# A scheduler's model of TensorE: other prices for weight matmuls and for fp32 matmuls

## The chip, the cores and the metric

The kernel is one program on one core of a Trainium2 chip. The metric is device time in microseconds, the median of three runs: 2716.33 before (2714.63 to 2718.19). The profile comes from an execution of its own, which took 2712.5 us, with a span of 2710.6 us from the first to the last instruction; of the difference of 1.9 us the records show nothing.

## What is computed

Two blocks run one after the other on 256 tokens of width 1024, with 256 context tokens in the first block. Cut to its outline (`silu` and the norms as usual):

```python
for i in range(2):                       # first block: two layers
    x, ctx = ffn(x), ffn(ctx)            # SwiGLU, hidden width 2816, half residual, adaptive norms
    if i == 0:
        oc, ox = deltanet(ctx, x)        # gated delta rule, 8 heads, chunks of 64, both directions
    else:
        oc, ox = window_attention(ctx, x)
    x = ffn(x + gate * ox)               # ctx too, in layer 0
u = rms_norm(x)                          # second block
proj = u @ w_in                          # one wide projection for three branches
y = gates * (conv_branch, ssd_branch, window_attention_branch)
x = x + merged(y) @ w_mix_out
x = x + cross_attention(rms_norm(x), norm(mem))     # keys and values from 256 memory tokens
x = x + relu(rms_norm(x) @ w_up)**2 @ w_down        # hidden width 4096
```

In the DeltaNet, each chunk of 64 needs the solution of a unit lower triangular system (`triangular_solve` in the reference).

## The kernel before

All weights are read once from HBM. Each product with a weight is made in three matmuls in fp32r (`mm3`): weight and activation are each split into a high and a low part, and high x high, high x low and low x high are added in PSUM. ScalarE makes the high part of a weight chunk and VectorE the low part (`split_w`: `CAST t<-raw` and `TENSOR_TENSOR t<-raw,t`). An fp32r matmul has 512 columns where context and tokens go together, 256 where there are tokens alone. Other matmuls, of the mixers, are in plain fp32; the trace shows two records for each of them.

**The order is made by a scheduler in the program** (`Driver`), while the program is built. Every engine has a clock in a table, `self.t`. Each instruction goes through `Engine.__getattr__`, line 191, which takes a price from `Engine.cost` and lets `Clocks.run` move the engine's clock; all instructions therefore stand at line 191 in the profile, and all DMAs at line 237, on one queue of SyncE that works in order. Work is written as generators ("streams") with priorities. `Driver.run` takes `now`, the clock of TensorE, and advances the first stream whose condition holds and whose `ready` time is not past `now`. Streams with `bg` (the splits, the substitution `dn_steps`, the convolution's `conv_taps`, rows of the modulation) go on while the clock of their own engine is at most 0.5 us ahead of `now`. Where no stream can go on, a job is taken: a piece of weight matmuls (`acc`, `tok_jobs`, `halves`). So jobs fill the time in which the streams wait, and the price of a matmul decides how many of them stand ahead of the next stream. Where there is neither, and `hot` is set, `keep_busy` issues a matmul of `ones` with the identity that serves nothing but the clock of TensorE; in `Clocks.run` a matmul costs double after a window with few columns.

**The stages of the trace**: start until 44 us, a feed-forward until 405, the DeltaNet until 868, feed-forwards until 1604, window attention until about 1764, a feed-forward until 1964, the three branches until about 2450, cross attention until 2521, the MLP until 2710.

Three places matter below.

- **DeltaNet.** `dn_prep(h)` stores the chunk matrices of a head to a scratch tensor in HBM (`ld`). `dn_subst(b)` loads those of four heads into a tile `bx` and starts `dn_steps(b)`, 62 VectorE instructions that solve four heads at once (`n<-bx,bx` and `bx<-bx,n`): block 0 for heads 0 to 3, block 1 for heads 4 to 7. `dn_store` writes the result to `xd`, from where `dn_head(h)` loads it (four DMAs a head, `t<-xd` and `t<-ld`) and goes on with small matmuls; `dn_chain` and `dn_out` run along the chunks of one head and direction, with VectorE instructions such as `s<-ps,dn_cKV`, and `out_jobs` multiplies with the output weight. In the middle `mem_norm` loads the memory tokens (`memT`), norms them, and `mem_k` offers 192 weight matmuls of 256 columns, for the cross attention much later, as filling work.
- **Window attention.** `tok_jobs` projects tokens; `att_q(j,t)` transposes queries that ScalarE, VectorE and GpSimd have normed and rotated.
- **Branches.** `conv_taps` runs the convolution's taps on VectorE (`xres<-t,c_late,xres`, two taps a step), `ssd_group(g)` prepares and `ssd_pair(g,j)` multiplies the state space branch; its factors come from VectorE (`t<-t,t` 128x512).

Of the kernel before, what the change touches and what calls it, by code (L numbers as in the profile page):

```python
# [106 lines left out]
class Clocks:  # L107
# [16 lines left out]
    def run(self, e, cost, ins, outs):  # L124

        rows = ins[0].shape[0] / P if ins else 1
        start = self.t[e]
        ins = [r for r in (region(a) for a in ins) if r]
        outs = [r for r in (region(a) for a in outs) if r]
        for rs, write in ((ins, False), (outs, True)):  # L130
            for tag, p0, p1, b0, b1 in rs:
                for q0, q1, c0, c1, t, f, w in self.log.get(tag, ()):
                    if (w or write) and q0 < p1 and p0 < q1 and c0 < b1 and b0 < c1:
                        start = max(start, t + self.hop(f, e))
        if e == "PE":

            tick = int(start / TICK)
            self.cols[tick] = self.cols.get(tick, 0) + cost * 2400 * rows
            if self.cols.get(tick - 1, 0) < 3060:
                cost *= 2  # L140
        self.t[e] = end = start + cost
        for rs, write in ((ins, False), (outs, True)):
            for tag, p0, p1, b0, b1 in rs:
                old = self.log.get(tag, ())
                keep = [o for o in old if not (p0 <= o[0] and o[1] <= p1 and b0 <= o[2] and o[3] <= b1
                                               and (write or not o[6] and o[5] == e))]
                self.log[tag] = keep[-40:] + [(p0, p1, b0, b1, end, e, write)]
        return end


class Engine:
# [5 lines left out]
    def cost(self, op, a, k):  # L157
        def size(ap):
            n = 1
            for s in ap.shape[1:]:  # L160
                n *= s
            return n

        n = size(k.get("out", a[0] if a else None))
        if self.name == "PE":
            if op == "transpose":
                return 0.12
            if a[2].dtype == F32R:
                return 0.0025 + max(n * 0.000417, 0.107)

            tiles = {32: 0.29, 64: 0.52}.get(a[0].shape[0], 1) if a[1].shape[0] == P else 1
            return 2 * max(n * 0.000833, 0.03) * tiles
        if self.name == "ACT":
            c = 0.093 * (1 + sum(hasattr(k.get(x), "tensor") for x in ("scale", "bias"))) + n * 0.000833
            f = k.get("func")
            if f in TABLES and not self.drv.has(f):
                self.drv.table = AF.Exp if f == AF.Tanh else f
                c += 1.28
            return c
        if self.name == "DVE":  # L180
            if op == "reciprocal":
                return 0.07 + n * 0.0063
            c = 0.061 * sum(hasattr(k.get(x), "tensor") for x in ("scalar", "scalar1", "scalar2"))
            return 0.068 + c + (size(k["in_"]) if op == "tensor_reduce" else n) * 0.00104
        return 0.1 + n * 0.0021
# [2911 lines left out]
```

## Time and profile before

| | us |
|---|---|
| median of three runs | 2716.33 |
| the profiled execution | 2712.5 |
| its span | 2710.6 |
| TensorE matmuls busy | 2633.4 (97%) |
| VectorE busy | 1928.1 (71%) |
| ScalarE busy | 1255.8 (46%) |
| GpSimd busy | 101.2 (4%) |
| mean granted clock of TensorE | 0.983 |

Engines work beside each other, so shares do not add up. A row of a timeline gives the start, the time from the first start to the last end, the instruction and how often; a bracket at its end is idle time of the engine ahead of it and what ended that. The chain of waits is followed back from the last instruction. The granted clock is 1 at 2.4 GHz and 0.5 at 1.2 GHz.

### The profile page before, as it was taken

What the parts mean: (1) busy time and instruction counts of PE and PEld (TensorE: products, weight loads), DVE (VectorE), ACT (ScalarE), POOL (GpSimd) and SP (SyncE); (2) the same over time, 40 slices, a digit from 0 to 9 for tenths busy, and PEclk for the clock granted to TensorE, in tenths of its full rate; (3) what the DMA queues carried; (4) which work ended last, traced back from release to release, by engine and by line L of the source; (5) the groups of instructions that cost most, each with busy time, mean ns of one, the idle gap of its engine ahead of it and who ended that gap; (6) DMA issues with size and microseconds to landing.
All of it is one profiled execution on the core that took longest, in us unless ns stands there. A gap on an engine that the chain in (4) does not pass through costs nothing.

```text
span 2710.6 us, 45364 instructions
## 1 busy us (share of the span) xinstructions
PE 2633.4 (97%) x17414; PEld 2330.9 (86%) x17414; DVE 1928.1 (71%) x3897; ACT 1255.8 (46%) x2799; POOL 101.2 (4%) x114
## 2 busy tenths in 40 slices
PE   7999999999789999999999998999999899999999
PEld 5888888887779888889888886899979789999999
DVE  6878767897768498875433367765688898886763
ACT  4323145754245323234423255654476676565652
POOL 0000000200010000000000001000010220000000
PEclk8999999999789999999999998999999999999999
DMA  8657723759433465672322221355554444554554
GB/s 317 210 195 261 253 94 124 243 185 263 121 122 110 150 214 206 241 248 78 111 100 93 93 101 55 105 195 183 173 170 155 150 170 159 182 191 150 179 194 134
DMA packets 194058, 452.57 MB, mean 167 GB/s; under 512 B 33472, under 2 KB 78624, under 8 KB 193840
## 3 DMA queue, kind: packets, MB, share of 16 engines
q1 hardware_dynamic: 193840, 449.66, 49.6%
q8 instruction: 137, 2.24, 0.3%
q14 instruction: 81, 0.66, 0.1%
HBM read 418.65 MB, written 30.94 MB: 166 GB/s over the span
## 4 chain that ended last, share of the span: by engine, by line
PE 90%; DVE 6%; ACT 2%; issue 1%; DMA 1%; POOL 0%; SPq 0%; DVEq 0%; POOLq 0%; ACTq 0%
PE ps L191 90%; DVE t L191 3%; ACT t L191 1%; DVE n L191 1%; DVE rs L191 1%; DVE s L191 1%; ACT s L191 1%; DVE xres L191 0%; DMA row<-in_ada_w 0%; DVE bx L191 0%; DMA xres<-in_xT 0%; ACT L191 0%; ACT n L191 0%; DVE acc L191 0%; DVE ps L191 0%
## 5 line engine op out<-in xcount | busy, mean ns | idle before, releaser
L191 PE MATMUL ps<-t,t 128*128 128x256 f32 (+4 forms) x14610 | 2373.5, 326 | 22.2 <-DVE t L191 13.3
L191 PEld LDWEIGHTS ps<-t,t 128*128 128x128 f32 (+2 forms) x14610 | 2077.4, 188 | 273.1 <-issue 25.8
L191 DVE TENSOR_TENSOR t<-raw,t 128x512 fp32r<-128x512 f32 x1124 | 735.4, 684 | 60.5 <-ACT t L191 54.2
L191 ACT CAST t<-raw 128x512 fp32r<-128x512 f32 x1124 | 630.3, 610 | 254.3 <-DMA raw<-in_ffn_w 188.3
L191 ACT CAST t<-t 128x512 fp32r<-128x512 f32 (+2 forms) x144 | 68.2, 493 | 426.6 <-DVE t L191 426.1
L191 DVE TENSOR_TENSOR t<-t,ps 128x512 f32<-128x512 f32 (+1 forms) x104 | 64.7, 628 | 234.4 <-PE ps L191 234.4
L191 DVE CUSTOM_DVE_ANT_0 t<-row,bx,c_early 128x1024 bf16<-128x1024 f32 x128 | 163.9, 1280 | 47.9 <-DMA row<-in_ada_r 47.4
L191 DVE SCALAR_TENSOR_TENSOR xres<-ps,modG,xres 128x256 f32<-128x256 f32 x216 | 97.2, 479 | 117.1 <-PE ps L191 116.3
L191 ACT ACTIVATE t<-ps 128x512 f32<-128x512 f32 (+3 forms) x161 | 75.0, 466 | 195.7 <-PE ps L191 182.7
L191 POOL TENSOR_TENSOR t<-t,c_late 128x512 f32<-128x512 f32 (+2 forms) x58 | 67.1, 1172 | 1715.2 <-ACT t L191 1094.9
L191 DVE CUSTOM_DVE_ANT_0 row<-row,bx,c_early 128x1024 f32<-128x1024 f32 x96 | 122.7, 1280 | 1.2
L191 DVE TENSOR_TENSOR t<-t,t 128x512 fp32r<-128x512 f32 (+4 forms) x174 | 95.1, 561 | 39.4 <-ACT t L191 38.9
L191 DVE SCALAR_TENSOR_TENSOR t<-ps,c_late,t 128x254 f32<-128x254 f32 (+3 forms) x176 | 111.9, 637 | 12.8 <-ACT t L191 7.3
L191 PE MATMUL ps<-s,t 128*128 128x128 f32 x512 | 87.7, 315 | 22.1 <-ACT t L191 10.0
L191 PEld LDWEIGHTS ps<-s,t 128*128 128x128 f32 x512 | 73.4, 215 | 32.6 <-ACT t L191 10.9
L191 ACT COPY t<-ps 128x512 f32<-128x512 f32 (+4 forms) x141 | 57.8, 435 | 93.5 <-PE ps L191 88.1
L191 DVE SCALAR_TENSOR_TENSOR xres<-t,c_late,xres 128x256 f32<-128x256 f32 x150 | 87.5, 583 | 3.1
L191 ACT ACT_TABLE_LOAD x58 | 74.4, 1283 | 2.7 <-PE ps L191 1.7
L191 PE MATMUL ps<-c_early,t 128*128 128x128 f32 (+1 forms) x374 | 59.9, 285 | 10.4 <-ACT t L191 6.0
L191 PEld LDWEIGHTS ps<-c_early,t 128*128 128x128 f32 (+1 forms) x374 | 43.7, 145 | 26.0 <-ACT t L191 13.6
L191 ACT ACTIVATE n<-xres 128x256 f32<-128x256 f32 x90 | 35.7, 414 | 59.8 <-DVE xres L191 58.4
L191 ACT ACTIVATE t<-ps,c_late 128x256 f32<-128x256 f32 (+1 forms) x64 | 37.6, 588 | 53.7 <-PE ps L191 53.6
(188 smaller groups left out, 1365.3 us busy)
## 6 DMA issues: line engine op xcount, KB each, us to landing
raw<-in_ffn_w SPq DMA_DIRECT2D x240, 512.0 KB, 4.2
row<-in_ada_r SPq DMA_DIRECT2D x128, 512.0 KB, 4.4
raw<-in_w_in SPq DMA_DIRECT2D x81, 512.0 KB, 3.5
raw<-in_dn_w SPq DMA_DIRECT2D x33, 512.0 KB, 4.0
raw<-in_w_up SPq DMA_DIRECT2D x32, 512.0 KB, 4.2
raw<-in_w_down SPq DMA_DIRECT2D x32, 512.0 KB, 5.5
raw<-in_ffn_w SPq DMA_DIRECT2D x32, 384.0 KB, 3.6
s<-t SPq DMA_DIRECT2D x32, 256.0 KB, 4.2
```

The costliest lines, as they stand in the source:

```text
L191: r = f(*a, **k)
```

## The change

Two formulas in `Engine.cost` get other numbers. In the scheduler's prices (not measured times) an fp32r matmul goes from 0.216 to 0.231 us at 512 columns and from 0.109 to 0.119 at 256, an fp32 matmul of 128 columns from 0.213 to 0.219, one of 32x32 from 0.060 to 0.055, and one of one column from 0.060 to 0.040.

```diff
@@ Engine.cost, engine PE
             if a[2].dtype == F32R:
-                return 0.0025 + max(n * 0.000417, 0.107)
+                return 0.006 + max(n * 0.0004395, 0.1)
             tiles = {32: 0.29, 64: 0.52}.get(a[0].shape[0], 1) if a[1].shape[0] == P else 1
-            return 2 * max(n * 0.000833, 0.03) * tiles
+            return 2 * max(n * 0.000855, 0.02) * tiles
```

No work is added or taken away but two of the matmuls of `keep_busy` (34 instead of 32). Only the order moves, and with it the buffers. Three places follow, each as it stands before and then as it stands in the change.

SyncE's queue in the DeltaNet, before, after the store of block 0's solution (`xd<-bx`); `ld_126` and `ld_127` are blocks 0 and 1 of the scratch tensor, and the rows behind it are the loads of heads 0 to 3, and after them `bx<-ld_127`.

```order
L237 DMA xd_128<-bx_4875 128x32x32
L237 DMA t_5778<-in_memT 128x512
L237 DMA t_5780<-in_memT 128x512
L237 DMA t_5782<-in_memT 128x512
L237 DMA t_5784<-in_memT 128x512
L237 DMA z_153<-t_5776 128x512
L237 DMA ld_127<-t_5741 128x4x128
L237 DMA ld_127<-t_5742 128x4x128
L237 DMA q_144<-t_5202 128x512
L237 DMA q_145<-t_5203 128x512
L237 DMA t_5809<-xd_128 128x4x128
L237 DMA t_5812<-xd_128 128x4x128
```

In the change, twelve loads of heads 0 to 2 and four weight loads and stores later, this piece begins with the fourth head.

```order
L237 DMA raw_5785<-in_xk_w 128x1024
L237 DMA t_5791<-xd_128 128x4x128
L237 DMA t_5794<-xd_128 128x4x128
L237 DMA t_5795<-ld_126 128x4x128
L237 DMA t_5796<-ld_126 128x4x128
L237 DMA t_5807<-in_memT 128x512
L237 DMA t_5809<-in_memT 128x512
L237 DMA t_5811<-in_memT 128x512
L237 DMA t_5813<-in_memT 128x512
L237 DMA z_153<-t_5805 128x512
L237 DMA ld_127<-t_5822 128x4x128
L237 DMA ld_127<-t_5823 128x4x128
```

The four loads of `memT` have moved from ahead of all sixteen loads of the heads to behind them. The load `bx<-ld_127` comes 36 rows into the piece that begins with the store in the change (26 before), behind six loads of head 0's later tiles that it had ahead of it before.

VectorE in the substitution of block 1, before: `n` and `bx` are its rows, `s` and `t` those of the chains of heads 0 to 3.

```order
L191 TENSOR_TENSOR n_6354<-bx_5954,bx_5955 128x192
L191 TENSOR_TENSOR bx_5955<-bx_5955,n_6354 128x24x8
L191 SCALAR_TENSOR_TENSOR s_6506<-ps_6491,dn_cA,t_5814 128x128
L191 TENSOR_SCALAR s_6510<-ps_6479,dn_cKV 128x128
L191 TENSOR_TENSOR n_6353<-bx_5954,bx_5955 128x207
L191 TENSOR_TENSOR bx_5955<-bx_5955,n_6353 128x23x9
L191 TENSOR_TENSOR n_6354<-bx_5954,bx_5955 128x220
L191 TENSOR_TENSOR bx_5955<-bx_5955,n_6354 128x22x10
L191 TENSOR_SCALAR t_5838<-ps_6316 64x4x64
L191 TENSOR_TENSOR n_6353<-bx_5954,bx_5955 128x231
L191 TENSOR_TENSOR bx_5955<-bx_5955,n_6353 128x21x11
L191 TENSOR_TENSOR n_6354<-bx_5954,bx_5955 128x240
```

In the change, from the same step (128x192) on:

```order
L191 TENSOR_TENSOR n_6201<-bx_6045,bx_6046 128x192
L191 TENSOR_TENSOR bx_6046<-bx_6046,n_6201 128x24x8
L191 TENSOR_SCALAR t_5772<-ps_6173 64x4x64
L191 TENSOR_SCALAR s_6375<-ps_6322,dn_cKV 128x128
L191 SCALAR_TENSOR_TENSOR t_5764<-ps_6219,dn_eg,t_5764 128x128
L191 TENSOR_TENSOR t_5764<-ps_6219,t_5764 128x128
L191 COPY n_5970<-ps_6357 32x128
L191 COPY n_5970<-ps_6358 32x128
L191 SCALAR_TENSOR_TENSOR t_5764<-ps_6263,dn_eg,t_5764 128x128
L191 TENSOR_TENSOR t_5764<-ps_6263,t_5764 128x128
L191 SCALAR_TENSOR_TENSOR s_6394<-ps_6381,dn_cA,t_5748 128x128
L191 SCALAR_TENSOR_TENSOR s_6398<-ps_6391,dn_cA,t_5761 128x128
```

Rows of the chains now stand between the steps in greater number. Between the first step of block 1 and its last stand 105 rows before and 166 in the change, 61 of them steps in both: 55 rows more of the chains of heads 0 to 3 and five more splits; after the last step 73 rows of those chains are left before, and 18 in the change. On TensorE, the filling matmuls of `mem_k` stand otherwise to the substitution of block 1: before, 102 of the 192 ahead of its first step, 39 between first and last and 51 behind (3 of these before the last instruction of the DeltaNet); in the change 12, 87 and 93 (45).

VectorE in the branches, before, ahead of the first factor of `ssd_pair` of group 0, which is the row `t_20963<-t_20963,t_20834`:

```order
L191 TENSOR_TENSOR t_21067<-raw_20907,t_21066 128x512
L191 SCALAR_TENSOR_TENSOR xres<-t_19925,c_late,xres 128x256 x2
L191 TENSOR_TENSOR t_21085<-raw_20953,t_21084 128x512
L191 TENSOR_TENSOR t_21108<-raw_20953,t_21107 128x512
L191 SCALAR_TENSOR_TENSOR xres<-t_19925,c_late,xres 128x256 x2
L191 TENSOR_TENSOR t_21133<-raw_21046,t_21132 128x512
L191 SCALAR_TENSOR_TENSOR xres<-t_19925,c_late,xres 128x256 x2
L191 TENSOR_TENSOR t_21158<-raw_21046,t_21157 128x512
L191 SCALAR_TENSOR_TENSOR xres<-t_19925,c_late,xres 128x256 x2
L191 TENSOR_TENSOR t_20963<-t_20963,t_20834 128x512
```

In the change, ahead of the same factor, here `t_20940<-t_20940,t_20829`:

```order
L191 SCALAR_TENSOR_TENSOR t_21024<-ps_20979,c_late,t_21024 128x255
L191 TENSOR_TENSOR t_21040<-raw_20879,t_21039 128x512
L191 TENSOR_TENSOR t_21058<-raw_20921,t_21057 128x512
L191 SCALAR_TENSOR_TENSOR t_21024<-ps_21019,c_late,t_21024 128x253
L191 SCALAR_TENSOR_TENSOR t_21024<-ps_21019,c_late,t_21024 128x254
L191 SCALAR_TENSOR_TENSOR t_21024<-ps_21019,c_late,t_21024 128x255
L191 TENSOR_TENSOR t_21084<-raw_20921,t_21083 128x512
L191 TENSOR_TENSOR t_21107<-raw_20977,t_21106 128x512
L191 TENSOR_TENSOR t_20940<-t_20940,t_20829 128x512
L191 TENSOR_TENSOR t_20943<-t_20943,t_20829 128x512
```

The four tap steps are gone from there: in both orders 30 tap rows are issued ahead of this factor, but in the change the last of them stands 31 rows ahead of it. What is left next to the factor are splits and the branch's own short convolution (`t<-ps,c_late,t`). Between this factor and the first one of group 1 stand 24 rows before and 35 in the change: six more splits, three more rows of the short convolution, two more tap rows.

## Rows read from the trace of the kernel before

**Rows 1.** The page: busy time of two engines' groups, and the chain of waits.

```profile
PE 2633.4 (97%) x17414; PEld 2330.9 (86%) x17414; DVE 1928.1 (71%) x3897; ACT 1255.8 (46%) x2799; POOL 101.2 (4%) x114
...
PE 90%; DVE 6%; ACT 2%; issue 1%; DMA 1%; POOL 0%; SPq 0%; DVEq 0%; POOLq 0%; ACTq 0%
```

**Rows 2.** TensorE by form: count, busy us, mean ns, idle before.

```profile
L191 PE MATMUL ps<-t,t 128*128 128x512 f32 x5448 | 1262.5, 392 | 0.6 <-ACT n L191 0.6
L191 PE MATMUL ps<-t,t 128*128 128x256 f32 x8136 | 1026.3, 287 | 8.1 <-DVE t L191 5.7 <-ACT t L191 2.2
```

**Rows 3.** Busy time by stretch: length, PE, PEld, DVE, ACT, POOL, granted clock, DMA.

```profile
50.00:100.00 50.00, 50.00 (x279) 43.89 (x278) 41.34 (x68) 16.33 (x30) 0.00 (x0) 1.00 0.67 247
...
667.70:707.90 40.20, 29.55 (x279) 26.88 (x278) 34.49 (x108) 9.82 (x31) 2.13 (x2) 0.76 0.26 88
707.90:813.00 105.10, 89.63 (x910) 78.73 (x909) 69.40 (x227) 45.90 (x168) 9.02 (x9) 0.88 0.45 139
813.00:868.40 55.40, 55.22 (x343) 49.01 (x343) 46.99 (x112) 29.77 (x77) 3.69 (x4) 1.00 0.31 105
1640.00:1703.00 63.00, 53.47 (x346) 36.34 (x344) 44.41 (x94) 32.57 (x78) 10.04 (x12) 0.89 0.12 42
```

**Rows 4.** Timeline of TensorE in the DeltaNet, around the norm of the memory.

```profile
615.79 4.47 PE L191 MATMUL ps<-t,t 128*128 128x512 f32 x19
620.10 1.05 PE L191 MATMUL ps<-t 128*128 128x128 f32 x8
...
622.58 9.13 PE L191 MATMUL ps<-c_early,ones 128*128 128x128 f32 x34
...
636.72 3.55 PE L191 MATMUL ps<-t,t 128*128 128x256 f32 x15
```

**Rows 5.** Timeline of SyncE's DMA queue, same place.

```profile
618.99 0.43 SPq L237 DMA_DIRECT2D xd<-bx  x1
619.51 5.78 SPq L237 DMA_DIRECT2D t<-in_memT  x4
...
629.50 1.45 SPq L237 DMA_DIRECT2D t<-xd  x2
...
643.36 0.83 SPq L237 DMA_DIRECT2D bx<-ld  x1
...
649.71 3.04 SPq L237 DMA_DIRECT2D t<-s  x4
```

**Rows 6.** Timeline of VectorE: the first step of block 1.

```profile
667.66 0.18 DVE L191 TENSOR_TENSOR n<-bx,bx 128x31 f32<-128x31 f32 x1
```

**Rows 7.** VectorE by form, 640 to 812 us: three forms of the chains, the splits.

```profile
L191 DVE TENSOR_SCALAR s<-ps,dn_cKV 128x128 f32<-128x128 f32 x45 | 15.0, 343 | 6.5 <-PE ps L191 6.3
...
L191 DVE TENSOR_TENSOR t<-ps,t 128x128 f32<-128x128 f32 x39 | 11.2, 287 | 1.9 <-ACT t L191 1.0
...
L191 DVE TENSOR_TENSOR t<-raw,t 128x512 fp32r<-128x512 f32 x12 | 8.0, 676 | 2.2 <-ACT t L191 2.2
```

**Rows 8.** Timeline of TensorE in the window attention.

```profile
1649.16 1.09 PE L191 MATMUL ps<-c_early,t 128*128 128x128 f32 x4 [4.37 <-DVE t L191]
...
1665.88 1.33 PE L191 MATMUL ps<-c_early,t 128*128 128x128 f32 x8 [0.96 <-ACT t L191]
1668.92 3.34 PE L191 MATMUL ps<-t,t 64*128 64x512 f32 x14 [1.72 <-DVE t L191]
```

**Rows 9.** Timeline of TensorE in the branches: groups 0 and 1 of `ssd_pair`.

```profile
2134.93 0.71 PE L191 MATMUL ps<-t,t 128*64 128x128 f32 x6 [3.63 <-DVE t L191]
...
2155.43 0.68 PE L191 MATMUL ps<-t,t 128*64 128x128 f32 x6 [3.28 <-issue]
```

**Rows 10.** Timeline of VectorE in the branches: two tap steps.

```profile
2122.06 2.41 DVE L191 SCALAR_TENSOR_TENSOR xres<-t,c_late,xres 128x256 f32<-128x256 f32 x2
...
2133.27 1.00 DVE L191 SCALAR_TENSOR_TENSOR xres<-t,c_late,xres 128x256 f32<-128x256 f32 x2
```

**Rows 11.** Timeline of GpSimd beside those taps: its first row.

```profile
2122.02 0.74 POOL L191 TENSOR_TENSOR n<-n,t 128x256 f32<-128x256 f32 x1 [92.87 <-ACT n L191]
```

## The prediction

> **What bounds the kernel now.** The page comes first: matmuls are busy for 2633.4 of 2710.6 us, and the chain of waits, followed back from the end, lies on TensorE for 90%, on VectorE for 6% [rows 1]. The forms then say what TensorE does: 5448 matmuls of 512 columns and 8136 of 256 are nearly all of it, and they hardly wait (0.6 and 8.1 us in all) [rows 2]. The busy time by stretch says where order can matter at all. In a feed-forward stretch TensorE is busy 50.00 of 50.00 us at a granted clock of 1.00 [rows 3]; there another order of the same matmuls costs nothing as long as it stays full, and some 2200 us are of this kind. The rest is a few stretches: the DeltaNet from the end of its projections at 620.1 to 868.4 (busy 29.55 of 40.20 and 89.63 of 105.10 us, at clocks of 0.76 and 0.88), the window attention (53.47 of 63.00, at 0.89) [rows 3], and two waits in the branches (3.63 and 3.28 us) [rows 9]. Only there can the change move the end.
>
> No instruction becomes faster. The pace itself can be read off: 19 matmuls of 512 columns from 615.79 take 4.47 us, the last for 0.392, so their starts are (4.47 - 0.392) / 18 = 0.227 us apart [rows 2, 4]. The old price was 0.216, the new one is 0.231; the new one is nearer. That alone is worth nothing: an order is paid for by the waits that it leaves.
>
> The Trainium skill speaks against the change at this point. "TensorE: Matmul & The Clock Gate", section "Wait — 56ns, not 53.3ns?", gives 215.7 ns from start to start for 512 columns, which is the old price. By it the new table would be the worse one and I would put ten points more on slower, while the sum would stay, since the order is fixed when the program is built. The trace has 227 ns, so the measurement decides for the new price.
>
> **The change, part by part.**
>
> *DeltaNet.* Before, the queue of SyncE stores block 0's solution at 618.99, spends 5.78 us on the memory tokens, and comes to the first load of a head at 629.50 and to block 1's load at 643.36. TensorE meanwhile has 34 records of `ones` matmuls from 622.58, and the first `mem_k` matmuls come at 636.72 [rows 4, 5]. In the change the heads' loads go first and the memory norm comes behind them. So heads 0 to 3 start earlier, the filling starts later, and block 1's substitution meets other neighbours. Heads 4 to 7 wait for that substitution, and the stage's end waits for them, so I follow it in three terms.
>
> (a) Its first step, now at 667.66 [rows 6]. Ahead of it 90 `mem_k` matmuls are gone from TensorE, at 1026.3 / 8136 = 0.126 us each 11.3 us [rows 2]; nine splits are gone from VectorE, at 0.676 us each 6.1 us [rows 7]. Against that, block 1's load stands behind six more loads on SyncE, four of which take 3.04 us, so six some 4.6 [rows 5]. From -11 to +5; I take -6, the splits, because the step is a VectorE instruction and those were in its own queue.
>
> (b) Its length, now 667.7 to 707.9. The 55 rows more of heads 0 to 3 are forms of 0.287 to 0.343 us, at 0.327 on average 18.0 us, and five splits are 3.4, together 21.4 [rows 7]. VectorE is busy for 34.49 of these 40.20 us, so at most 5.7 us of it find idle time [rows 3]: from +16 to +21. I take +18: some of the idle time is a wait for TensorE that stays.
>
> (c) What follows it, 707.9 to 868.4. The same 55 rows of VectorE are missing there: -18.0 if VectorE set the pace. TensorE loses 65 matmuls of the chains; an fp32 matmul of 128 columns is two records at 1.05 / 8 = 0.13 us [rows 4], so 17.1 us, and gets 42 more `mem_k` matmuls, 5.3 us: -11.8. If heads 4 to 7 only wait for their own chains, nothing comes back. From -18 to 0; TensorE is busy there for 89.63 + 55.22 of 160.5 us, VectorE for 69.40 + 46.99 [rows 3], so I take TensorE's figure: -12.
>
> Together -6 + 18 - 12 = 0, and with the ends that hurt or help at once -11 + 16 - 18 = -13, or +5 + 21 - 9 = +17, where (c) returns half of VectorE's figure.
>
> *Window attention.* Before, TensorE is full until 1644.8, then waits 4.37 us for the transposes of `att_q` [rows 8]. In the change these transposes stand two groups of three matmuls earlier. The wait begins 6 x 0.227 = 1.4 us earlier and ends when it did, and these six come behind it. They are lost if nothing later waits, and found again if they fill the waits of 0.96 and 1.72 us that follow [rows 8]. From -1 to +4 (a longer wait can bring the half clock once more; the stretch has 0.89 already [rows 3]). I take +1.4.
>
> *Branches.* Before, the factor of `ssd_pair` in group 0 stands on VectorE behind four tap steps of two taps, the last of which starts at 2133.27, and TensorE waits 3.63 us for it until 2134.93 [rows 9, 10]. The change puts all four steps ahead of the preparation of the group. If the factor then comes a wait earlier, -3.6. But VectorE is nearly full there, and a tap step put earlier pushes what stood there. In group 1 eleven more rows stand ahead of the factor, six splits of 0.676 and five short ones, some 6 us in VectorE's queue, against 3.28 us of wait now [rows 7, 9]: +3, from 0 to +6. Together -0.6, from -4 to +5.
>
> A tap step takes 2.41 us while GpSimd works, from 2122.02 on, and 1.00 us after it has ended [rows 10, 11]. The Trainium skill, "SBUF — State Buffer", section "SBUF: two separate sides", names a port pair of the two engines that one of them holds for a whole instruction. By it steps moved ahead of GpSimd's run would cost 1.0 each, and three of them would save VectorE 4 us; the sum for the branches would be about -4. No row shows when the moved steps will run, so I leave it at the bound.
>
> *The rest.* Two more `keep_busy` matmuls stand where TensorE waits anyway: nothing. The norms between the stages start some matmuls later, in full stretches: nothing, and the waits behind them stay.
>
> **Sum.** 0 + 1.4 - 0.6 = +0.8 us: from the profiled 2712.5 to 2713.3, and since the median of the runs stands 3.8 us above the profiled one, 2717. That is no change that a measurement of this kernel can tell, which takes some 0.2%, 5.4 us.
>
> **The rivals.**
>
> *Tail relieved, faster.* Heads 0 to 3 use the hole from 622 to 637 and are done when heads 4 to 7 start. For it: all of the work of (c) is really gone from the tail, filling lies beside it, and the clock there is only 0.88. Against it: heads 4 to 7 depend on block 1, which (b) delays. With all low ends in the DeltaNet, -13, and the rest as above: 2716.3 - 12 = 2704.
>
> *Block 1 pays in full, slower.* If its load is late by the loads ahead of it and its 62 steps share VectorE with the chains throughout, (a) is +5, (b) +21, (c) only -9: +17, 2716.3 + 18 = 2734. For it: VectorE is busy 86% there. It decides from a first step later than about 666, with a last step later than 725.
>
> *The waits only change places, slower by a little.* Window attention and group 1 take their upper ends (+4 and +6, with nothing won in group 0): 2716.3 + 10 = 2726. For it: both lie behind engines whose work did not shrink.
>
> *Nothing moves that counts.* The order differs in names of buffers and in filling alone, and the waits last what they did: 2716. It ends as the forecast does, and is counted with it.
>
> **How the numbers follow.** Forecast, with the last rival: 0.38. Relieved tail: 0.30. Block 1 in full: 0.20. Waits change places: 0.12. So faster 0.30, same 0.38, slower 0.32. The range reaches to the time of either far rival and two or three us beyond, since either can fall on both sides of its figure: 2701 to 2736. The forecast's own range is 2711 to 2722, the bound of 5.4 us on either side.
>
> **What would show it.** (a) The first small `n<-bx,bx` row, at about 662 where this is right. (b) The last one some 58 us later, about 720. (c) From it to the end of the stage about 150 us instead of 160. In the window attention the wait ahead of the four transposes at about 5.7 instead of 4.37 us. In the branches no wait of over a microsecond ahead of group 0, and one of 3 to 6 us ahead of group 1. The feed-forward stretches should stay at 50.00 of 50 us. I am wrong if one of these shows a gap, or if block 1's substitution ends earlier than before: then VectorE had more room than its busy share says.

## The result, and the profile after

The changed kernel takes 2752.1 us (2751.07 to 2754.76, four runs) against 2715.48 before (2713.93 to 2718.19): a ratio of 1.0132 [1.012, 1.0144], 36.6 us slower. The forecast was 2717, its range ended at 2736, and the truth lies outside. The profiled execution took 2754.76 us, 2.7 above the median, where that of before stood below its own; so the two traces differ by 42.3 us in span, somewhat more than the medians.

The page of the changed kernel, busy time and the chain of waits, which answer to [rows 1]:

```profile
span 2752.9 us, 45377 instructions
...
PE 2657.6 (97%) x17418; PEld 2352.0 (85%) x17418; DVE 1921.0 (70%) x3897; ACT 1259.8 (46%) x2803; POOL 102.8 (4%) x114
...
PE 55%; issue 31%; DVE 8%; ACT 3%; DMA 3%; SPq 0%; POOL 0%; DVEq 0%; ACTq 0%; POOLq 0%
```

Two sums can be read off. TensorE's idle time is span less busy time: 77.2 us before, 95.3 now, so 18.1 of the 42.3 us are new waits. The other 24.2 us are busy time, with the same number of matmuls but four: the work did not grow, it ran longer, and the mean granted clock fell from 0.983 to 0.971. Where it fell differs by stage, as the stretches below show. In the chain, "issue" has 31% instead of 1%; it names no culprit, and idle rows tell more.

TensorE by form, as in [rows 2]:

```profile
L191 PE MATMUL ps<-t,t 128*128 128x512 f32 x5448 | 1269.6, 393 | 9.3 <-ACT t L191 8.3 <-DVE t L191 1.0
L191 PE MATMUL ps<-t,t 128*128 128x256 f32 x8136 | 1031.8, 287 | 7.2 <-DVE t L191 3.9 <-ACT t L191 3.1
```

The matmuls of 512 columns waited 0.6 us in all before and wait 9.3 now. That is the first surprise: most of them belong to the feed-forwards, the full stretches. Busy time by stretch, as in [rows 3] (length, PE, PEld, DVE, ACT, POOL, clock, DMA share, GB/s); first the feed-forward after the DeltaNet and 50 us out of it, then the DeltaNet up to block 1's first step, its steps, and what follows, then the window attention, and last the whole DeltaNet behind its projections and a piece of it:

```profile
880.00:1258.10 378.10, 369.08 (x1782) 311.47 (x1781) 281.38 (x496) 112.91 (x216) 0.00 (x0) 0.99 0.56 196
1100.00:1150.00 50.00, 43.58 (x182) 35.21 (x181) 40.80 (x72) 13.17 (x24) 0.00 (x0) 0.93 0.64 228
625.80:670.00 44.20, 38.50 (x358) 32.62 (x357) 26.38 (x66) 15.57 (x46) 2.17 (x2) 0.58 0.96 273
670.00:730.70 60.70, 54.23 (x503) 50.91 (x503) 51.79 (x169) 20.08 (x62) 2.08 (x2) 0.83 0.21 70
730.70:880.00 149.30, 141.13 (x1201) 123.94 (x1200) 103.65 (x288) 70.89 (x231) 12.73 (x12) 0.89 0.45 140
1640.00:1703.00 63.00, 53.70 (x259) 38.39 (x259) 40.92 (x82) 33.56 (x86) 10.28 (x14) 0.92 0.22 76
...
625.80:880.00 254.20, 233.86 (x2058) 207.47 (x2057) 181.82 (x520) 106.53 (x337) 16.98 (x16) 0.82 0.48 147
633.20:670.70 37.50, 33.09 (x299) 28.67 (x300) 22.16 (x56) 13.12 (x42) 2.17 (x2) 0.50 0.91 259
```

The same two stages in the trace of before, the feed-forward and the DeltaNet:

```profile
868.40:1233.70 365.30, 365.30 (x1790) 310.05 (x1789) 283.24 (x498) 114.63 (x216) 0.00 (x0) 1.00 0.59 203
622.70:868.40 245.70, 217.55 (x2029) 190.63 (x2028) 180.70 (x514) 107.69 (x336) 17.32 (x16) 0.90 0.49 148
```

In the DeltaNet TensorE does not wait longer, it waits less: length less busy time is 28.2 us before and 20.3 now. Its busy time rose by 16.3 us, two thirds of the 24.2, for nearly as many records (2029 and 2058), and the clock fell from 0.90 to 0.82. From 633.2 to 670.7 it was at half clock throughout, busy for 33.09 of 37.50 us with the small matmuls of the heads and, until 656.9, without a weight matmul. So this stage pays in clock and not in waits.

The feed-forward after the DeltaNet, full before from end to end (365.30 of 365.30 us), has 9.02 us of gaps. Where most of them are, by TensorE's timeline:

```profile
976.95 0.50 PE L191 MATMUL ps<-t,t 128*128 128x512 f32 x1 [1.94 <-ACT t L191]
...
1083.82 26.45 PE L191 MATMUL ps<-t,t 128*128 128x512 f32 x116
1116.33 0.80 PE L191 MATMUL ps<-t,t 128*128 128x512 f32 x1 [6.06 <-ACT t L191]
```

The releaser is ScalarE's `t`; back from it, on ScalarE and VectorE:

```profile
1115.66 0.62 ACT L191 CAST t<-t 128x512 fp32r<-128x512 f32 x1 [8.64 <-DVE t L191]
```

```profile
1101.29 1.28 DVE L191 CUSTOM_DVE_ANT_0 t<-row,bx,c_early 128x1024 bf16<-128x1024 f32 x1 [2.55 <-DMA row<-in_ada_r]
...
1110.27 1.28 DVE L191 CUSTOM_DVE_ANT_0 t<-row,bx,c_early 128x1024 bf16<-128x1024 f32 x1 [0.47 <-DMA row<-in_ada_r]
...
1113.73 1.28 DVE L191 CUSTOM_DVE_ANT_0 t<-row,bx,c_early 128x1024 bf16<-128x1024 f32 x1 [0.23 <-DMA row<-in_ada_r]
...
1114.94 0.68 DVE L191 TENSOR_TENSOR t<-t,ps 128x512 f32<-128x512 f32 x1
```

So a load of the modulation's weights (`row<-in_ada_r`) is late; VectorE stands 2.55 us at an instruction that nobody is in a hurry for; behind it in the same queue stands the feed-forward's product (`t<-t,ps`), which ends at 1115.62; ScalarE casts it, and TensorE, out of other work, has waited 6.06 us. The page gives those loads 4.1 us from issue to landing (before: 4.4). The scheduler's price for 512 KB is 0.5243 MB at 360 GB/s, 1.46 us, plus `DMA_LAT`, 0.75 us: 2.2 us.

### The profile page after: what moved, and what is told of

Same layout as the page of the kernel before. It is cut to its first block, busy times and chain, and to the rows that moved or that the text cites. A ratio compares the mean times of both kernels' runs of the same rounds, so it can differ in the third digit from the quotient of the medians.

```text
span 2752.9 us, 45377 instructions
## 1 busy us (share of the span) xinstructions
PE 2657.6 (97%) x17418; PEld 2352.0 (85%) x17418; DVE 1921.0 (70%) x3897; ACT 1259.8 (46%) x2803; POOL 102.8 (4%) x114
## 4 chain that ended last, share of the span: by engine, by line
PE 55%; issue 31%; DVE 8%; ACT 3%; DMA 3%; SPq 0%; POOL 0%; DVEq 0%; ACTq 0%; POOLq 0%
PE ps L191 55%; DVE t L191 4%; ACT t L191 2%; DVE rs L191 1%; DVE n L191 1%; ACT L191 1%; DMA row<-in_ada_r 1%; DVE xres L191 1%; DVE bx L191 0%; DMA t<-xd 0%; DVE s L191 0%; DVE row L191 0%; DMA t<-band 0%; DMA raw<-in_ffn_w 0%; DMA raw<-in_ada_w 0%
## 5 line engine op out<-in xcount | busy, mean ns | idle before, releaser
L191 PE MATMUL ps<-t,t 128*128 128x256 f32 (+3 forms) x14610 | 2392.3, 328 | 42.2 <-DVE t L191 19.1
L191 DVE CUSTOM_DVE_ANT_0 t<-row,bx,c_early 128x1024 bf16<-128x1024 f32 x128 | 164.1, 1282 | 72.7 <-DMA row<-in_ada_r 72.5
L191 ACT ACTIVATE s<-ps,dn_cV 128x128 f32<-128x128 f32 x64 | 22.7, 369 | 81.6 <-DVE s L191 64.8
```

The costliest lines, as they stand in the source:

```text
L191: r = f(*a, **k)
```

## The experiments

The tables below give, for each kernel, its time, that of the kernel before on the same chip, and by how much each stage is longer than in the trace of before (us, worked out from the first and the last weight matmul of the stages). Lengths before: the first feed-forward with the projections of the DeltaNet 586.5, the DeltaNet behind them 245.7, the feed-forward after it 365.3, window attention 129.7, the branches up to their gates 298.4, and on to the cross attention 188.7. "Rows" is VectorE's whole wait for `row<-in_ada_r`. In the first two columns of stages part of a difference is scatter: e17 and e18 have the old order word for word up to the branches, and show up to 7.5 us in the one and 4.2 in the other, but at most 1.1 in the next two. Most kernels ran once, and 19 executions of the kernel before on one chip took 2709.28 to 2728.68 us; so a difference of less than some 10 us between two single times says little, and the stages say more.

In the expectations, **M** (margin) says that the too cheap matmul kept the other engines ahead of TensorE; **F** that the fp32 price does it; **R** (rough) that the old order is a good one among many and any other loses; **L** (landing) that the loads' price is too low and the cheap matmul covered for it.

| kernel | time | before | first ffn, proj. | DeltaNet | ffn after | window | branches | on | rows |
|---|---|---|---|---|---|---|---|---|---|
| before | | | | | | | | | 47.4 |
| the change | 2752.1 | 2715.5 | +4.2 | +8.5 | +12.8 | +7.5 | +9.8 | +0.3 | 72.5 |
| e1 | 2759.5 | 2721.2 | +9.1 | +15.6 | +13.1 | +7.8 | +5.5 | +0.4 | 61.9 |
| e2 | 2718.3 | 2721.2 | +4.0 | -1.6 | -0.4 | +4.2 | +1.7 | 0 | 49.2 |
| e3 | 2756.5 | 2721.2 | +4.4 | +10.7 | +1.3 | +7.3 | -6.1 | +28.6 | 38.6 |
| e4 | 2745.3 | 2721.2 | +4.0 | +11.9 | +6.6 | +7.9 | +4.7 | +1.0 | 61.0 |
| e7 | 2730.7 | 2715.8 | +0.3 | +3.0 | +7.4 | -0.1 | +7.1 | 0 | 72.1 |
| e9 | 2712.7 | 2715.8 | +0.9 | -1.0 | +2.5 | +3.3 | -3.7 | 0 | 47.2 |
| e5 | 2738.2 | 2715.8 | +4.3 | +3.2 | +9.6 | +4.2 | +5.7 | +0.3 | 65.9 |
| e10 | 2738.0 | 2715.8 | +7.3 | +4.8 | -0.6 | +6.3 | +10.0 | +0.3 | 18.9 |
| e8 | 2751.9 | 2715.2 | +14.2 | +4.8 | +14.4 | +4.1 | +3.0 | +0.3 | 69.2 |
| e12 | 2765.3 | 2717.3 | +7.4 | +19.1 | +11.8 | +8.8 | +7.9 | +0.3 | 67.0 |
| e13 | 2747.5 | 2717.3 | +3.7 | +18.0 | +0.4 | +8.8 | +7.8 | +0.3 | 22.9 |
| e11 | 2728.5 | 2717.3 | +4.2 | +1.7 | -0.9 | +6.5 | +1.9 | +0.3 | 24.8 |
| e16 | 2748.7 | 2717.0 | +8.9 | +12.1 | +1.8 | +5.1 | +8.6 | +0.4 | 31.4 |
| e14 | 2715.1 | 2717.3 | +1.7 | +4.0 | 0 | +1.6 | -4.2 | 0 | 16.4 |
| e15 | 2725.7 | 2717.0 | +3.1 | +4.1 | -0.9 | +6.6 | +3.0 | +0.3 | 21.5 |
| e19 | 2725.8 | 2715.2 | +6.3 | +4.3 | -0.9 | +6.3 | +0.6 | +0.3 | 23.8 |
| e17 | 2716.3 | 2717.0 | +7.5 | +3.8 | +1.1 | -0.1 | -3.1 | 0 | 54.2 |
| e18 | 2716.2 | 2717.0 | -0.2 | +4.2 | +0.4 | 0 | -8.1 | +8.3 | 45.7 |

### Which of the two prices (e1, e2)

The two lines of the change, one at a time; e1 has the fp32r line alone, e2 the fp32 line alone.

```diff
-                return 0.0025 + max(n * 0.000417, 0.107)
+                return 0.006 + max(n * 0.0004395, 0.1)
```

> Only the weight matmuls get the new price (0.231 for 0.216 us at 512 columns, 0.119 for 0.109 at 256); the fp32 price is the old one. Theory M (margin: the old price of weight matmuls was some 5% below the 0.227 us of the trace, so VectorE, ScalarE and the DMAs got 5% more time than the scheduler meant, and the change takes this away): 2740 to 2755, nearly the whole loss. Theory F (the fp32 price did it, by the small matmuls of the DeltaNet): 2712 to 2720. Theory R (rough: the old order is a good one among many, and any other price lands 20 to 45 us above it): 2735 to 2760.

```diff
-            return 2 * max(n * 0.000833, 0.03) * tiles
+            return 2 * max(n * 0.000855, 0.02) * tiles
```

> Only the fp32 matmuls get the new price (0.219 for 0.213 us at 128 columns, 0.040 for 0.060 at one column); weight matmuls keep the old one. Theory M: 2710 to 2722, since the filling work is not repriced. Theory F: 2740 to 2755. Theory R: 2735 to 2760.

Measured: 2759.53 and 2718.26 us against 2721.15. The fp32r price carries the whole loss; the fp32 price is worth nothing that one run shows. F falls.

### The price as a dose (e3, e4, e7, e9)

For 512 columns, e3 has 0.201 us, e9 0.214, before 0.216, e7 0.218, e4 0.2235, the change 0.231. The lines of the four, in this order:

```diff
+                return 2 * (0.0025 + max(n * 0.000417, 0.107)) - (0.006 + max(n * 0.0004395, 0.1))
...
+                return 0.99 * (0.0025 + max(n * 0.000417, 0.107))
...
+                return 1.01 * (0.0025 + max(n * 0.000417, 0.107))
...
+                return 0.5 * (0.0025 + max(n * 0.000417, 0.107)) + 0.5 * (0.006 + max(n * 0.0004395, 0.1))
```

> The weight matmuls are repriced by the same amount to the other side (0.201 us at 512 columns, 0.100 at 256), fp32 as before; the order again differs everywhere. Theory M: more margin, so no new waits on TensorE in the feed-forwards and the branches, 2700 to 2722. Theory R: the direction does not matter, 2735 to 2760. This run tells M from R.

> Old prices, weight matmuls 1% cheaper (0.214 us at 512 columns). Theory M: 2710 to 2720. Theory R: 2735 to 2760. Mixed: the feed-forwards at zero, DeltaNet and window attention together +5 to +20; 2720 to 2740.

> Old prices, weight matmuls 1% dearer (0.218 us at 512 columns). Theory M: 2714 to 2724. Theory R: 2735 to 2760 though the price is nearly the same. Mixed: the feed-forwards and the branches as before within 3 us, DeltaNet and window attention together +5 to +20; 2720 to 2740.

> The weight matmuls get the mean of old and new price (0.2235 us at 512 columns, 0.114 at 256), fp32 as before. Theory M: about half the loss, 2725 to 2740. Theory R: not ordered by price, anywhere from 2735 to 2760.

Two stages follow the price roughly, though not step by step. In the feed-forward after the DeltaNet: +1.3, +2.5, 0, +7.4, +6.6, +12.8 from the lowest price to the highest. In the branches up to their gates: -6.1, -3.7, 0, +7.1, +4.7, +9.8. Dearer matmuls lose in both stages, and so much of M holds; cheaper ones gain only in the branches, since the feed-forward was full already. The total does not follow: the cheapest price is as bad as the change, 2756.48 us, because a stage that the others leave alone takes 28.6 us more. TensorE there in e3:

```profile
2428.18 1.01 PE L191 MATMUL ps<-ones,acc 128*128 128x1 f32 x4 [9.14 <-DVE acc L191]
...
2439.86 1.02 PE L191 MATMUL ps<-ones,acc 128*128 128x1 f32 x4 [9.18 <-DVE acc L191]
```

Two norms wait over 9 us each for VectorE. And a step of 1% upwards (e7) costs 15 us in one run, 7.4 and 7.1 of them in the two stages named, and 1% down (e9) nothing measurable in one run. That much of R holds: among the six prices tried, only the old one and the one 1% below it are fast.

### Relative price or landing (e5, e10, e8)

If it were the ratio of TensorE's price to the others', raising the others by 6.7% would nearly bring the old feed-forward back. Nearly, because the change raises TensorE's price by 6.9% at 512 columns and 8.2% at 256. The price of landing stays out of it. e5 is the change, and

```diff
-            self.drv.end(self.drv.clk.run(self.name, self.cost(op, a, k), ins, outs))
+            self.drv.end(self.drv.clk.run(self.name, self.cost(op, a, k) * (1 if self.name == "PE" else 1.067), ins, outs))
...
-        t = self.clk.run("DMA", max(n / 360e3, 0.06), [in_], [out]) + DMA_LAT
+        t = self.clk.run("DMA", 1.067 * max(n / 360e3, 0.06), [in_], [out]) + DMA_LAT
```

> The change, and beside it the prices of VectorE, ScalarE, GpSimd and of DMA transfers raised by 6.7%, as the weight matmuls were, so that their ratio is about the old one again. Theory M (margin): the loss of the feed-forward after the DeltaNet (+12.8 us with the change) and of the branches (+9.8) goes; 2715 to 2730. Theory R (rough: any order but the old one loses): 2740 to 2760. Mixed (M in the feed-forward and the branches, R in the DeltaNet with +8 to +16 and in the window attention with +4 to +8): 2725 to 2740.

e10 is the change, with the modulation's rows, and only them, taken to land 2 us later:

```diff
-                drv.dma(w, self.A["ada_r"][i, c])
+                drv.end(drv.dma(w, self.A["ada_r"][i, c]) + 2.0)
```

> The change, but the scheduler is told that a row of the modulation weights lands 2 us later than its price says (2.2 us then become 4.2, and the page has 4.1 from issue to landing), so that VectorE's instruction on the row is ordered behind more other work. If the feed-forward's +12.8 us come from VectorE standing at rows that have not landed (72.5 us of such waits against 47.4 before): that wait total falls below 50 us, the two waits of TensorE at 975 and 1110 us go, 2738 to 2744. If the rows only happen to stand there: no difference, 2750 to 2756. Theory R: 2735 to 2765, with no tie to that wait.

e8 is the change with twice the slack at every hand-over between streams:

```diff
-LAT = 0.2
+LAT = 0.4
```

> The change, with every hand-over between streams at 0.4 us instead of 0.2 and the landing as it was. Theory L (landing): little help for a row that lands 2 us late, the feed-forward keeps +6 to +12; 2740 to 2756. Any slack will do: the feed-forward and the branches fall as with the landing, 2720 to 2735.

The three tell the theories apart in the feed-forward after the DeltaNet: ratio nearly restored, still +9.6; hand-overs doubled, +14.4; landing corrected, -0.6. VectorE's wait for the rows (in all, times, longest) in the change, in e8 and in e10, and e10's feed-forward as busy time:

```profile
DVE t L191 <- DMA row<-in_ada_r: 72.5, 52, 5.0
```

```profile
DVE t L191 <- DMA row<-in_ada_r: 69.2, 56, 4.2
```

```profile
DVE t L191 <- DMA row<-in_ada_r: 18.9, 21, 2.1
```

```profile
880.00:1245.00 365.00, 365.00 (x1785) 309.41 (x1784) 282.89 (x496) 114.81 (x218) 0.00 (x0) 1.00 0.60 203
```

With the new price kept, the stretch is full again. The other runs agree. All six at the change's fp32r price with the rows priced 1 or 2 us later (e10, e13, e11, e16, e15, e19) are within -0.9 and +1.8 of before in this stage, all five without (the change, e1, e5, e8, e12) lose 9.6 to 14.4. VectorE's wait for the rows inside this stage alone sorts all 20 kernels too: up to 32.7 us in thirteen, none of which loses more than 2.5, and 38.2 us or more in seven, which lose 6.6 to 14.4. Before and in the change it is:

```profile
DVE t L191 <- DMA row<-in_ada_r: 28.0, 34, 3.7
```

```profile
DVE t L191 <- DMA row<-in_ada_r: 42.0, 31, 5.0
```

In this stage the cause is shown: the scheduler priced the rows as there about two microseconds before they were. How the cheap matmul had hidden it is argued and not measured: a given time on the scheduler's clocks then meant more time on the chip. L holds here. M as a matter of ratio is not supported, but e5 alone does not exclude it, since it restored the ratio only nearly and 1% (e7) was enough for +7.4. In total e10 gains 14 us of the 37 and leaves the rest where it was.

### The landing of all loads (e11, e16, e14)

The same correction for every DMA: on the change 2.75 (e11) and half of that, 1.75 (e16); e14 has 2.75 on the kernel before, as a control.

```diff
-DMA_LAT = 0.75
+DMA_LAT = 2.75
```

> The change, but every DMA lands 2 us later in the scheduler's account (0.75 us behind its transfer becomes 2.75). Theory L (what the change uncovers are prices of DMA landings that are too low; the cheap matmuls had covered them): the feed-forward's +12.8 goes as with the rows alone, and the branches' +9.8 fall to at most +4, since one of their waits follows from a load of 6.2 us; DeltaNet 0 to +10; 2718 to 2736. Theory R: 2735 to 2765, with losses in other stages.

> The old matmul prices and every DMA 2 us later in the account, the control for the run above. Theory L: little to gain where nothing waits, 2708 to 2722. Theory R (the old order is a good one, any other price loses): 2725 to 2760, above all in the DeltaNet and the window attention.

> The change with every DMA 1 us later in the scheduler's account (1.75 us behind the transfer; with 2 us more it was 2728.5). Theory L (late landing): in between, 2730 to 2745, with VectorE's wait for modulation rows between 25 and 72 us. Theory R (rough): no order by dose, 2725 to 2760 with losses elsewhere.

e11 comes to 2728.51 us, 24 below the change: the feed-forward is repaired, the branches have +1.9 instead of +9.8. e14 stays within 2.2 us of before, so it is no gain of its own: the landing price costs something only where the matmul price no longer covers it. e16 was expected between the two and is not: its feed-forward is repaired (+1.8), but its total is 2748.73, with +12.1 in the DeltaNet and +8.6 in the branches. Outside the feed-forward the landing price acts like any other number: it gives another order, and the order decides. That the branches' loss is landing too is therefore not shown.

### The DeltaNet's late filling (e12, e13)

The change puts the memory norm, and with it the `mem_k` filling, behind the loads of the heads, and TensorE then ran at a granted clock of 0.58 ahead of block 1. e12 is the change with the old place: heads wait until the memory tokens' loads are issued. e13 adds e10's line.

```diff
-        while self.flight >= self.heads:
-            yield lambda: self.flight < self.heads
+        while self.flight >= self.heads or not self.memed:
+            yield lambda: self.flight < self.heads and self.memed
...
-        return nrm.hl, lambda: drv.spawn(gen(), prio=6)
+        return nrm.hl, lambda: drv.spawn(gen(), prio=6 if tags else 1)
```

> The change, but in the DeltaNet the loads of the memory tokens are put back ahead of all loads of heads 0 to 3 (the heads wait until these are issued), so that the memory norm and the filling matmuls of mem_k come early again, as before. If the DeltaNet's +8.5 us come from the filling being late, so that only small matmuls stand on TensorE at half clock between 633 and 671: half clock in that stage falls from 92 to 50 to 65 us and the stage loses 5 to 9 us less; 2743 to 2748. If the substitution of block 1 (60.7 us long with the change, 40.2 before) sets the end whatever fills: 2750 to 2756. Other stages as with the change.

> Rows of the modulation 2 us later for the scheduler, and the memory tokens loaded first, both on the change. If the two causes are separate: the sum of both effects, -14 and -5 to -9, so 2729 to 2734. What is left above the old kernel is then the window attention and the branches, 14 to 18 us. If each edit only reshuffles: anywhere from 2735 to 2760.

In e12, by stretch, up to block 1's first step and behind its last:

```profile
630.30:668.40 38.10, 32.66 (x282) 25.86 (x282) 23.32 (x54) 13.00 (x32) 0.00 (x0) 0.87 0.93 251
...
716.70:895.10 178.40, 157.93 (x1330) 139.65 (x1331) 120.06 (x350) 77.91 (x253) 14.28 (x13) 0.90 0.41 123
```

The clock is back (0.87 for 0.58) and the first step comes 6.1 us earlier than in the change (38.1 us for 44.2 after the projections), and yet the stage is longer than in any other run, 19.1 us above before: what follows the last step takes 178.4 us instead of 149.3. The heads started later and ended later: counted from the end of the projections, their first load is issued 2.3 us later than in the change and the last one 24 us later. The whole stage in e12:

```profile
630.30:895.10 264.80, 226.71 (x2060) 198.50 (x2060) 183.81 (x520) 107.92 (x337) 17.60 (x16) 0.88 0.47 141
```

Busy time went down, as expected (226.71 us for 233.86), but TensorE now waits 38.1 us where it waited 20.3. So this edit gave back clock and cost more in waits. That the late filling alone makes the loss, so that undoing it gains 5 to 9 us, falls; how much of the change's +8.5 is the half clock this run cannot tell, since it moved the heads too. e13 repeats both halves: +0.4 in the feed-forward, +18.0 in the DeltaNet.

### Window attention (e15, e19)

What stays in e11 lies mostly in the window attention, +6.5. e15 is e11 with the old fp32r price while that stage is scheduled, e19 is e11 with 0.4 us at hand-overs there.

```diff
+                return 0.0025 + max(n * 0.000417, 0.107) if self.drv.stage else 0.006 + max(n * 0.0004395, 0.1)
...
+            drv.stage = "swa"
```

> The change with DMA landings 2 us later (2728.5), and in the window attention alone the old price of weight matmuls. If the price inside that stage does the +6.5: the stage is back within 2 us of the old one, 2720 to 2725. If the state at its start does it, or any order but the old one loses there: still +4 to +9, 2725 to 2732.

```diff
-        ev.t = max(self.fin, self.base) + LAT
+        ev.t = max(self.fin, self.base) + self.lat
...
+            drv.lat = 0.4
```

> The change with DMA landings 2 us later (window attention +6.5), and in the window attention alone each hand-over between streams taken as 0.4 us instead of 0.2, so that more filling stands ahead of each step. If that stage waits because its hand-overs are priced too low: +3 us or less there, about 2725. If not, +5 to +9, 2726 to 2735.

+6.6 and +6.3: neither the fp32r price inside the stage nor its hand-overs make the loss alone. That it comes with the state in which the stage is entered is what is left, but it is not shown: the new fp32 price stayed in force inside the stage, and e2, which has only that price, is at +4.2 there. With e1 at +7.8 under the old fp32 price, that price is not needed for the loss either. The cause stays open.

### Can the branches' gain be had alone (e17, e18)

e3 and e14 had been quicker in the branches. e17 is the kernel before with 2 us more of landing from the branches on, e18 the kernel before with e3's price up to the gates.

```diff
-        t = self.clk.run("DMA", max(n / 360e3, 0.06), [in_], [out]) + DMA_LAT
+        t = self.clk.run("DMA", max(n / 360e3, 0.06), [in_], [out]) + DMA_LAT + (2.0 if self.stage else 0.0)
...
+        self.do(lambda: setattr(drv, "stage", "mix"))
```

> The old prices; DMA landings 2 us later only from the start of the three branches on, so the order before them is the old one word for word. Theory L: the branches lose waits on loads, 3 to 6 us less than the old kernel, 2710 to 2713 against 2716. Theory R: 2716 to 2735.

```diff
-                return 0.0025 + max(n * 0.000417, 0.107)
+                return 2 * (0.0025 + max(n * 0.000417, 0.107)) - (0.006 + max(n * 0.0004395, 0.1)) if self.drv.stage else 0.0025 + max(n * 0.000417, 0.107)
...
+                self.do(lambda: setattr(drv, "stage", None))
```

> The old prices; weight matmuls 0.201 us at 512 columns only in the branches and only until the last gates' jobs. With the cheaper price everywhere this part of the branches was 6.1 us shorter than in the old kernel. If margin does it: 2709 to 2713. If that came from the state at the stage's start: 2714 to 2730.

Ten runs each: ratios 0.999 [0.9972, 1.0009] and 0.9999 [0.9987, 1.0012]. No gain. e18 wins 8.1 us in the branches and gives 8.3 back behind them. No version here beats the kernel before by more than a measurement can tell.

## Why the prediction was wrong

**The first step failed.** "[A]nother order of the same matmuls costs nothing as long as it stays full, and some 2200 us are of this kind", and of the few other stretches: "Only there can the change move the end." The condition was taken for granted for the 2200 us, on the strength of one full stretch in [rows 3]. A full TensorE does not say by how much the work ahead of it is early. The feed-forward after the DeltaNet lost 12.8 us, the largest single piece, and no rival had it; the stretches that the sum put at nothing hold 16.5 of the 42.3 us between the two traces. The prediction's own sign of being wrong came true here: "The feed-forward stretches should stay at 50.00 of 50 us", and the one from 1100 to 1150 has 43.58. The row that could have warned was in the waits of before: VectorE waited 28.0 us for `row<-in_ada_r` in that stage, two thirds of the 42.0 now, and TensorE still had work all the while (365.30 of 365.30 us). Both numbers of the cause were at hand, 4.4 us to landing on the page of before and 2.2 in the program. That one wrong price can be the cover of another was not thought of. This third of the loss has a shown cause; for the DeltaNet, the window attention and the branches the traces show where the time goes, and why stays in part open.

**A second step failed in the DeltaNet.** "[A]n order is paid for by the waits that it leaves" held in the feed-forward, where 9.0 of the 12.8 us are waits. In the DeltaNet the waits fell by 7.8 us and the busy time rose by 16.3, at a clock of 0.82 for 0.90. Half clock was given no term there; the prediction named it only as a chance for the window attention.

**The DeltaNet**, sum 0 (-13 to +17), measured +8.5, of which some 4 is within scatter. Block 1's first and last step in the change, as in [rows 6]:

```profile
670.05 0.18 DVE L191 TENSOR_TENSOR n<-bx,bx 128x31 f32<-128x31 f32 x1
...
730.52 0.19 DVE L191 TENSOR_TENSOR bx<-bx,n 128x31 f32<-128x31 f32 x1
```

(a) was to be about 662 and is 670.05; counted from the end of the projections, which themselves end later, the step moved by -0.7 where -6 stood. This term was mis-sized: the splits taken out of VectorE's queue did not bring the step forward. Part of what stands there in their place can be read off: the sixteen VectorE rows of the memory norm, of which eight are shown, before and in the change (duration in ns; first and last start):

```profile
L191 DVE SCALAR_TENSOR_TENSOR n<-t,c_late,ps x8: 472/474/481, 634.1 to 639.2; 128x256 f32<-128x256 f32 x8
```

```profile
L191 DVE SCALAR_TENSOR_TENSOR n<-t,c_late,ps x8: 473/475/481, 656.0 to 664.7; 128x256 f32<-128x256 f32 x8
```

They ended some 27 us ahead of the step before, and lie right ahead of it in the change, 7.6 us of work for all sixteen against the 6.1 us of splits that are gone. The prediction moved the norm but did not count its rows. In e12 the step comes 6.1 us earlier than in the change, but there the norm and the filling stand earlier and the heads later at once, so which of them held it is not told apart; block 1's load did not, since it is issued 25 us after the projections in both. (b) 60.7 us instead of 40.2, +20.5 where +18 (+16 to +21) stood: right. (c) 149.3 instead of 160.5, -11.2 where -12 stood: right. The three as measured add up to the stage's loss. The rival "Block 1 pays in full" had its two signs come true (after 666, after 725), but not its sum, since (c) returned more than it gave.

**Window attention**, +1.4 (-1 to +4), measured +7.5. TensorE there, as in [rows 8]:

```profile
1672.54 1.09 PE L191 MATMUL ps<-c_early,t 128*128 128x128 f32 x4 [4.80 <-DVE t L191]
...
1694.76 3.75 PE L191 MATMUL ps<-t,t 64*128 64x512 f32 x20 [2.72 <-DVE t L191]
...
1709.58 1.11 PE L191 MATMUL ps<-c_early,t 128*128 128x128 f32 x4 [3.15 <-ACT t L191]
```

The wait that was followed grew, by less than said (4.80 for 4.37, where 5.7 stood). The loss is further down: 2.72 us where 1.72 stood, and 3.15 us in a place where the stage of before has no wait above 0.97. In all TensorE is idle in this stage for 15.2 us instead of 9.7. The prediction held the later waits to be as they were and possibly filled. It looked at one wait and not at what would stand beside the following ones.

**Branches**, -0.6 (-4 to +5), measured +9.8. The first matmuls of `ssd_pair` in groups 0 to 3, as in [rows 9]:

```profile
2161.86 0.71 PE L191 MATMUL ps<-t,t 128*64 128x128 f32 x6 [0.47 <-DVE t L191]
...
2191.53 1.18 PE L191 MATMUL ps<-t,t 128*64 128x128 f32 x6 [5.15 <-DVE t L191]
...
2242.51 1.18 PE L191 MATMUL ps<-t,t 128*64 128x128 f32 x6 [4.58 <-DVE t L191]
...
2272.03 1.15 PE L191 MATMUL ps<-t,t 128*64 128x128 f32 x6 [3.32 <-issue]
```

Groups 0 and 1 came as forecast: under a microsecond instead of 3.63, and 5.15 where 3 to 6 stood. Groups 2 and 3, which waited 1.35 us and hardly at all before, were not looked at, and with 7.9 us of waits they are most of the loss; what makes them wait is open. VectorE ahead of group 1's factor, and GpSimd beside it:

```profile
2177.67 1.53 DVE L191 SCALAR_TENSOR_TENSOR xres<-t,c_late,xres 128x256 f32<-128x256 f32 x3
...
2184.55 2.39 DVE L191 SCALAR_TENSOR_TENSOR xres<-t,c_late,xres 128x256 f32<-128x256 f32 x2
2186.86 1.75 DVE L191 TENSOR_TENSOR t<-raw,t 128x512 fp32r<-128x512 f32 x1
2188.53 2.34 DVE L191 SCALAR_TENSOR_TENSOR xres<-t,c_late,xres 128x256 f32<-128x256 f32 x2
2190.80 0.68 DVE L191 TENSOR_TENSOR t<-t,t 128x512 f32<-128x512 f32 x1
```

```profile
2180.94 0.74 POOL L191 TENSOR_TENSOR n<-n,t 128x256 f32<-128x256 f32 x1 [17.82 <-ACT n L191]
...
2189.16 1.44 POOL L191 TENSOR_TENSOR t<-t,c_late 128x512 f32<-128x512 f32 x1
```

Before GpSimd's run three taps take 1.53 us, within it two take 2.39, and a split 1.75 instead of 0.68. The Trainium skill, "SBUF — State Buffer", section "SBUF: two separate sides", gives the two engines a shared port pair that one holds for a whole instruction; this trace agrees, as [rows 10, 11] did. By these rows and the 1.00 us of a tap step in [rows 10], two tap steps and a split beside GpSimd cost (2.39 - 1.00) + (2.34 - 1.00) + (1.75 - 0.68) = 3.8 us more, most of that wait of 5.15. No run here moved them away, so it is a reading and not shown.

## What to carry to other kernels

A scheduler's prices are right or wrong together: a matmul of 512 columns priced 5% too low was the cover of loads priced 2 us too low, and correcting the one laid the other bare, so a price that seems wrong by itself is best corrected together with those that lean on it. Here that mended one stage and not the kernel: with both prices corrected (e11) it took 2728.5 us, 11 more than the kernel before. Before calling a stretch safe because its engine is full, read the waits of the engines that feed it: a queue in order that already waits for loads (28.0 us in the stage that lost most) can be a loss that has not arrived yet. And an order of this kind can hang on little: 1% on one price cost 15 us in one run, so after a truer price the whole order has to be timed again.

## What the runs showed of the hardware that was not expected

The page's row for the loads concerned, before and in the change (KB each, us to landing):

```profile
row<-in_ada_r SPq DMA_DIRECT2D x128, 512.0 KB, 4.4
```

```profile
row<-in_ada_r SPq DMA_DIRECT2D x128, 512.0 KB, 4.1
```

A load of this size lands 4.1 us after its issue in the change, almost three times the 1.46 us that the scheduler counts for its bytes. The Trainium skill, "DMA: Bandwidth & Descriptors", section "Anatomy of one DMA — SWDGE (gpsimd) path", gives a DMA of GpSimd's queue a fixed part of about 2.0 us beside its bytes, and by its fit 512 KB would take an estimated 3.2 us; the loads here are SyncE's, and the trace has the larger figure. And the same order does not take the same time everywhere: e17 and e18 have the old order up to the branches, and their stages there differ from the trace of before by up to 4.7 us (the first feed-forward alone; 7.5 with the projections behind it) and 4.2 us (the DeltaNet), while the feed-forward after it agrees within 1.1 us and the window attention within 0.1. One trace says little about differences of that size in those two stages, and several terms of the prediction were smaller.

Half clock can cost more than the waits do: in the change TensorE was at half clock from 633.2 to 670.7 us though it was busy for 33.09 of these 37.50 us, with small matmuls; up to block 1's first step the change has 12 weight matmuls behind the projections and a clock of 0.58, e12 has 48 and 0.87.
